# Down projection of a decoder layer: twelve of 22 feature blocks of each half as Strassen products

## The chip, the cores and the metric

The kernel runs on one core of a Trainium2 chip. The engines are named as the profile names them: PE (TensorE, matmuls), DVE (VectorE), ACT (ScalarE), POOL (GpSimd) and SP (the queue that issues most loads). The metric is the device time of one execution in microseconds (us).

## The reference

One decoder layer on 256 tokens of width 2048, float32 throughout: two attention groups side by side, then a feed-forward part of width 5632 and a final norm. The change is in the last product, `@ w_down`.

```python
    x = x + jnp.concatenate([o_mla, o_nsa], axis=-1) @ w_o[l]
    h = rmsnorm(x, ffn_norm_g[l])
    x = x + (jax.nn.silu(h @ w_gate[l]) * (h @ w_up[l])) @ w_down[l]
return rmsnorm(x, final_norm_g)
```

## The kernel before, in words

Products of float32 are made of three matmuls of `float32r` values: each operand is a pair (hi, lo), and hi x hi, hi x lo and lo x hi are added up in a PSUM bank. Weights come as tiles of 128 x 1024 float32. The class `Stream` handles them in the order in which PE takes them: `_dma` loads a tile on SP's queue into `wraw` (three buffers), `_split` copies it on ACT into `whi` (L143) and subtracts that copy from the tile on DVE into `wlo` (L145). In the attention part POOL takes the last 256 columns of the subtraction (L147, `W.share = 256`); from the feed-forward part on DVE takes all of it (`W.share = 0`). A split is one or two tiles ahead of PE.

The feed-forward part runs in two halves of 22 blocks of 128 features (`NFH = 22`). In a half, gate and up are made for each block (`gate_up`, L214 and L215), and `activate` turns their banks into silu(gate) * up, split into `aT`. Then the down projection of that half runs over four column groups `dg` of 512 columns. A weight tile holds two feature blocks x 512 columns; a group takes 11 tiles, and each tile has 12 matmuls of 512 columns (two token halves t, two feature blocks, three products; L856 to L858). The two banks of a group are added to x on DVE (L873). In the second half each finished group is squared and multiplied by `gfin` on POOL (L879); for the last group the second token half is held back by four tiles, so that the first one's output is under way while PE still works.

PE's order is written out by hand in `program()`. The orders on the other engines are set by a scheduler; each engine works its queue in order.

## Time and profile before

| | |
|---|---|
| Median of the runs shown (three) | 1088.46 us (1087.44 to 1089.93) |
| Span of the profiled execution | 1087.1 us, 16200 instructions |
| First and second down projection | 119.72 us and 120.77 us |
| PE busy over the span | 1061.6 us, 98% |
| DVE, ACT, POOL busy over the span | 645.5, 563.3 and 203.8 us |

The profiled execution's own time stands only as its span; the median lies 1.4 us above it. A group of instructions is given by its line, engine, operation, the tiles written and read, its shape, count, busy time and mean duration in ns. Matmuls are pipelined, so a matmul's duration is longer than the time from one start to the next; the pace is read from counts in a window.

### The profile page before, as it was taken

To read this page: it belongs to the slowest core of one execution; us is meant where nothing else is said; L and a number is where in the kernel's file an instruction comes from. 1 tells how busy PE (TensorE), PEld (TensorE's weight loads), DVE (VectorE), ACT (ScalarE), POOL (GpSimd) and SP (SyncE) were. 2 spreads that over 40 slices of the span, in tenths; PEclk is the share of its full clock that TensorE was granted. 3 is DMA by queue.
4 is the path that set the end of the run, shared out by engine and by line. 5 is a ranking of instruction groups with operands and counts; after the bars stand their busy time and mean duration, and the time that the engine had idled before them with its cause. 6 is when DMAs were issued, how large, how long until landed. Compare 5 with 4: busy or idle time off the path is not lost.

```text
span 1087.1 us, 16200 instructions
## 1 busy us (share of the span) xinstructions
PE 1061.6 (98%) x6102; PEld 927.9 (85%) x6102; DVE 645.5 (59%) x1016; ACT 563.3 (52%) x993; POOL 203.8 (19%) x206
## 2 busy tenths in 40 slices
PE   7989999899999999999999999999999999999996
PEld 7989998778888888888888888888888888888885
DVE  4557989886556555555555544455555555555554
ACT  5647887854455544454544333344444444444442
POOL 1144444533343010101011000001010010101110
PEclk9989999999999999999999999999999999999999
DMA  8844443324456555555555555555555555556553
GB/s 275 268 136 157 142 133 98 99 97 135 136 169 214 187 187 192 193 191 185 190 191 193 193 194 194 194 186 184 194 179 189 186 186 191 182 189 193 194 194 134
DMA packets 54543, 193.57 MB, mean 178 GB/s; under 512 B 6404, under 2 KB 6660, under 8 KB 54336
## 3 DMA queue, kind: packets, MB, share of 16 engines
q1 hardware_dynamic: 54000, 191.36, 53.6%
q0 software_dynamic: 464, 1.17, 0.3%
q8 instruction: 48, 0.79, 0.3%
q14 instruction: 31, 0.25, 0.1%
HBM read 190.41 MB, written 2.10 MB: 177 GB/s over the span
## 4 chain that ended last, share of the span: by engine, by line
PE 89%; DVE 4%; ACT 3%; issue 1%; DMA 1%; SPq 0%; POOL 0%; POOLq 0%; DVEq 0%; ACTq 0%
PE up L214 15%; PE gate L214 15%; PE gate L215 8%; PE up L215 8%; PE dn L857 7%; PE dn L858 7%; PE dn L856 7%; PE woM L745 1%; PE woM L746 1%; PE woM L747 1%; PE woN L745 1%; PE woN L747 1%; PE woN L746 1%; PE ps_q L219 1%; DVE wlo L145 1%
## 5 line engine op out<-in xcount | busy, mean ns | idle before, releaser
L145 DVE TENSOR_TENSOR wlo<-wraw,whi 128x1024 fp32r<-128x1024 f32 (+3 forms) x351 | 417.0, 1188 | 386.6 <-ACT whi L143 385.4
L143 ACT CAST whi<-wraw 128x1024 fp32r<-128x1024 f32 (+2 forms) x351 | 366.1, 1043 | 448.1 <-PE dn L858 127.8
L214 PE MATMUL gate<-h2T,whi 128*128 128x512 f32 x704 | 248.7, 395 | 0.0
L214 PE MATMUL up<-h2T,whi 128*128 128x512 f32 x704 | 248.5, 395 | 0.0
L215 PE MATMUL gate<-h2T,wlo 128*128 128x256 f32 x704 | 197.7, 281 | 0.0
L215 PE MATMUL up<-h2T,wlo 128*128 128x256 f32 x704 | 197.7, 281 | 0.0
L824 POOL TENSOR_TENSOR u<-t,RB 128x512 f32<-128x512 f32 x44 | 57.0, 1296 | 556.7 <-DVE t L823 556.7
L214 PEld LDWEIGHTS up<-h2T,whi 128*128 128x128 f32 x704 | 132.0, 187 | 30.8
L214 PEld LDWEIGHTS gate<-h2T,whi 128*128 128x128 f32 x704 | 132.0, 188 | 30.7
L857 PE MATMUL dn<-wlo,aT 128*128 128x512 f32 x352 | 137.2, 390 | 0.6 <-DVE wlo L145 0.6
L858 PE MATMUL dn<-whi,aT 128*128 128x512 f32 x352 | 137.1, 390 | 0.0
L856 PE MATMUL dn<-whi,aT 128*128 128x512 f32 x352 | 137.1, 389 | 0.0
L215 PEld LDWEIGHTS gate<-h2T,wlo 128*128 128x128 f32 x704 | 133.2, 189 | 0.1
L215 PEld LDWEIGHTS up<-h2T,wlo 128*128 128x128 f32 x704 | 133.2, 189 | 0.0
L147 POOL TENSOR_TENSOR wlo<-wraw,whi 128x256 fp32r<-128x256 f32 x70 | 88.6, 1266 | 143.2 <-ACT whi L143 118.2
L857 PEld LDWEIGHTS dn<-wlo,aT 128*128 128x128 f32 x352 | 66.1, 188 | 14.7 <-DVE wlo L145 1.0
L856 PEld LDWEIGHTS dn<-whi,aT 128*128 128x128 f32 x352 | 66.1, 188 | 13.8
L858 PEld LDWEIGHTS dn<-whi,aT 128*128 128x128 f32 x352 | 66.1, 188 | 13.6
L219 PE MATMUL ps_q<-hT,whi 128*128 128x256 f32 x128 | 38.1, 297 | 0.5 <-ACT RB L210 0.5
L220 PE MATMUL ps_q<-hT,whi 128*128 128x256 f32 x128 | 36.7, 287 | 0.0
L221 PE MATMUL ps_q<-hT,wlo 128*128 128x256 f32 x128 | 36.7, 287 | 0.0
L745 PE MATMUL woN<-whi,oT 128*128 128x512 f32 x64 | 26.7, 417 | 0.2 <-ACT oT L548 0.2
(322 smaller groups left out, 1491.6 us busy)
## 6 DMA issues: line engine op xcount, KB each, us to landing
wraw<-in_w_dram SPq DMA_DIRECT2D x338, 512.0 KB, 3.5
wraw<-in_g_dram SPq DMA_DIRECT2D x15, 440.0 KB, 5.0
x<-in_x_dram SPq DMA_DIRECT2D x4, 512.0 KB, 5.6
out_dram<-x SPq DMA_DIRECT2D x8, 256.0 KB, 2.6
xt<-in_xT_dram SPq DMA_DIRECT2D x3, 512.0 KB, 5.3
gfin<-in_gfin_dram POOLq DMA_DIRECT2D x1, 1024.0 KB, 5.9
xt<-in_xT_dram SPq DMA_DIRECT2D x1, 384.0 KB, 5.4
cst<-in_c_dram SPq DMA_DIRECT2D x1, 320.0 KB, 4.5
```

Of the source, the lines that this page charges most:

```text
L143: nc.scalar.copy(hi[:, c0:c1], raw[:, c0:c1])
L145: nc.vector.tensor_sub(lo[:, c0:c2], raw[:, c0:c2], hi[:, c0:c2].bitcast(F32))
L147: nc.gpsimd.tensor_sub(lo[:, c2:c1], raw[:, c2:c1], hi[:, c2:c1].bitcast(F32))
L214: nc.tensor.matmul(ps[0:hi.shape[1], :], hi, act, start=start, stop=False)
L215: nc.tensor.matmul(ps[0:hi.shape[1], 0:S], lo, act[:, 0, :], start=False, stop=stop)
L219: nc.tensor.matmul(ps, hi, act[:, 0, :], start=start, stop=False)
L220: nc.tensor.matmul(ps, hi, act[:, 1, :], start=False, stop=False)
L745: nc.tensor.matmul(pts[t], h_, wh, start=first, stop=False)
L824: nc.gpsimd.tensor_mul(u, t2, RB[:, None, :].to_broadcast([P, 2, S]))
L856: nc.tensor.matmul(pts[t], h_, wh, start=f == 0, stop=False)
L857: nc.tensor.matmul(pts[t], h_, wl, start=False, stop=False)
L858: nc.tensor.matmul(pts[t], l_, wh, start=False, stop=f == NFH - 1)
```

## The change

Of the 22 feature blocks of each half, blocks 0 to 11 become three steps of four blocks. A step takes the activations of its four blocks as a 2 x 2 arrangement A (token half x pair of blocks) and two column groups of the weights as a 2 x 2 arrangement B (pair of blocks x column group). The four block products of a step used to be eight products of a 128-token half with a weight tile; now they are seven, with four sums of weight tiles (P1 to P4) and four sums of activations (s1 to s4). Three of the weight sums are made on POOL, P2 on DVE. The sums are then split into hi and lo as loaded tiles are. Blocks 12 to 21 stay plain; their matmuls go into the same banks as the products. A pass `p` covers two column groups, and the eight banks are one set m1 to m8, of which m1, m5, m6 and m7 are combined with each other (`combine`) and all are added to x. The eight banks are in use in every pass. `whi` has four buffers instead of three, the tiles of the feed-forward part five instead of three; the sums have three of their own. `oT` moves to the pool of the attention part to make room. In the second half gate uses the banks S0 and O. The `gfin` tile is loaded in the second half.

```diff
+NS = 3
+UNITS = ("B11", "P1", "P3", "P2", "B22", "P4", "B21")
+LOADS = {"B11": (0, 0), "P1": (0, 1), "P3": (1, 1), "P4": (1, 0)}
+SUMS = {"P1": ("B11", "B12"), "P3": ("B12", "B22"), "P2": ("P1", "B22"), "P4": ("P2", "B21")}
+RAW_OF = {"B11": "B11", "P1": "B12", "P3": "B22", "P4": "B21"}
+A11, A12, A22, S1, S2, S3, S4 = range(7)
+PLAIN = (2, 4), (3, 8)
+PRODUCT = {"B11": (A11, 1), "P1": (S1, 5), "P3": (S3, 7), "P2": (S2, 6), "B22": (S4, 3), "P4": (A22, 4), "B21": (A12, 2)}
+def down_units(h, p):
+    plain = [("w", ("down", h, 2 * p + c, j)) for j in range(2 * NS, NFH // 2) for c in range(2)]
+    s = []
+    for i in range(NS):
+        for u in UNITS:
+            s.append(("sw", u, h, p, i))
+            if u in (("B11",) if i == NS - 1 else ("B11", "P1", "P2")):
+                s.append(plain.pop(0))
+    return s + plain
...
-        s += [("w", ("down", h, dg, j)) for dg in range(4) for j in range(NFH // 2)]
+        s += [u for p in range(2) for u in down_units(h, p)]
...
+            pool, tag, bufs = self.raws
+            if i - bufs in self.live:
+                return
...
+    def _sum(self, upto):
+        while self.na < min(upto, len(self.units)):
+            u = self.units[self.na]
+            if u[0] == "w":
+                self.parts[self.na] = self._take()
+            else:
+                what, at = u[1], u[2:]
+                if what in RAW_OF:
+                    r = RAW_OF[what]
+                    self.parts[at, r, "i"], self.parts[at, r] = self._take()
+                if what in SUMS:
+                    x, y = (self.parts[at, n] for n in SUMS[what])
+                    t = self.parts[at, what] = self.pool.tile([P, 1024], F32, tag="wraw", name=f"{what}_{self.na}", bufs=3)
+                    eng = self.nc.vector if what == "P2" else self.nc.gpsimd
+                    eng.tensor_add(t, x, y)
+                    if what == "P3":
+                        self._spent(at, "B12")
+                self.parts[self.na] = None, self.parts[at, what]
+            self.na += 1
...
-                    hi, lo = (self.pool.tile([P, 1024], F32R, tag=f"w{n}", name=f"w{n}{i}", bufs=3)
...
+                hi = self.pool.tile([P, 1024], F32R, tag="whi", name=f"whi{i}", bufs=4)
+                lo = self.pool.tile([P, 1024], F32R, tag="wlo", name=f"wlo{i}", bufs=3)
...
+        self._dma(self.nr + self.DMA_AHEAD)
+        self._sum(i + (self.SUM_AHEAD if unit[0] == "sw" else self.SPLIT_AHEAD))
...
+    NN = NFH - 4 * NS
+    aN = fp.tile([P, NN, 2, S], F32R, name="aN")
+    aS = fp.tile([P, NS, 2, 2, 7, P], F32R, name="aS")
+    W.raws = (fp, "raw", 5)
...
+        one, two = st["a", f % 4 - 2], v
+        a11, a21, a12, a22 = one[:, 0:P], one[:, P:S], two[:, 0:P], two[:, P:S]
+        c = temp(f"c_{h}_{f}").rearrange("p (b s) -> p b s", b=4)
+        s1, s2, s3, s4 = (c[:, b, :] for b in range(4))
+        nc.gpsimd.tensor_sub(s1, a22, a21)
+        nc.gpsimd.tensor_sub(s3, a11, a21)
+        nc.gpsimd.tensor_add(s2, a11, s1)
+        nc.gpsimd.tensor_sub(s4, a12, s2)
+        dst = aS[:, f // 4, f % 2]
+        split(dst[:, 0, A11, :], dst[:, 1, A11, :], a11)
+        split(dst[:, 0, A12:A22 + 1, :], dst[:, 1, A12:A22 + 1, :], two.rearrange("p (b s) -> p b s", b=2))
+        split(dst[:, 0, S1:, :], dst[:, 1, S1:, :], c)
...
+        W.DMA_AHEAD = 5
+        if h == 1:
+            gfin = hp.tile([P, D], F32, tag="big", name="gfin")
+            nc.gpsimd.dma_start(gfin, a["gfin"])
+        for p in range(2):
+            two = bank2(f"m67_{h}{p}")
+            tags = ("S0", "O", "ds", "ds") if h == 0 else ("ds", "ds", "S0", "O")
+            m = {6: two[:, 0, :], 7: two[:, 1, :]}
+            m |= {n: bank(t, f"m{n}_{h}{p}") for n, t in zip((1, 5, 3, 4), tags)}
+            m |= {n: bank("PT", f"m{n}_{h}{p}") for n in (2, 8)}
+            cols = [slice((2 * p + c) * 512, (2 * p + c + 1) * 512) for c in range(2)]
...
+                    h_, l_ = left(k)
+                    nc.tensor.matmul(m[to], h_, wh, start=first and k == 0, stop=False)
+                    nc.tensor.matmul(m[to], h_, wl, start=False, stop=False)
+                    nc.tensor.matmul(m[to], l_, wh, start=False, stop=last and k == 1)
...
+            def combine():
+                e, u, v, w = (temp(f"e{n}_{h}{p}") for n in range(4))
+                nc.scalar.copy(e, m[1])
+                nc.gpsimd.tensor_add(x11, x11, e)
+                nc.vector.tensor_sub(u, e, m[6])
+                nc.vector.tensor_add(w, u, m[5])
+                nc.gpsimd.tensor_sub(x12, x12, w)
+                nc.vector.tensor_add(u, u, m[7])
+                nc.vector.tensor_add(v, u, m[5])
+                nc.gpsimd.tensor_add(x21, x21, u)
+                nc.gpsimd.tensor_sub(x22, x22, v)
...
+                if unit[0] == "sw":
+                    form, to = PRODUCT[unit[1]]
+                    i = unit[4]
+                    mms(to, w, lambda k: [aS[:, i, k, b, form, :] for b in range(2)])
+                    if unit[1] == "B21" and i == NS - 1:
+                        combine()
...
+            if not end:
+                for xs, b in ((x11, 2), (x21, 4), (x12, 3), (x22, 8)):
+                    nc.vector.tensor_add(xs, xs, m[b])
+                if h == 1:
+                    for t in range(2):
+                        final(t, (2 * p, 2 * p + 1))
+                continue
```

POOL's queue at the turn from gate and up to the first down projection. `u` is the activation's product with the row scales, `P1` to `P4` are weight sums with the unit's number, `wraw` are loaded tiles. Before:

```order
L824 TENSOR_TENSOR u_0_19_6248<-t2_0_19_6247,RB_70 128x512
L824 TENSOR_TENSOR u_0_20_6350<-t2_0_20_6349,RB_70 128x512
L824 TENSOR_TENSOR u_0_21_6452<-t2_0_21_6451,RB_70 128x512
L824 TENSOR_TENSOR u_1_0_7360<-t2_1_0_7359,RB_70 128x512
L824 TENSOR_TENSOR u_1_1_7462<-t2_1_1_7461,RB_70 128x512
```

That is the whole of POOL's queue there: from one half's last activation straight to the next half's first. The same place in POOL's queue now:

```order
L905 TENSOR_TENSOR u_0_20_6405<-t2_0_20_6404,RB_70 128x512
L198 TENSOR_TENSOR P3_182_6561<-wraw180_6484,wraw182_6527 128x1024
L198 TENSOR_TENSOR P4_186_6605<-P2_183_6563,wraw184_6543 128x1024
L905 TENSOR_TENSOR u_0_21_6507<-t2_0_21_6506,RB_70 128x512
L198 TENSOR_TENSOR P1_190_6659<-wraw185_6575,wraw187_6633 128x1024
L198 TENSOR_TENSOR P3_192_6701<-wraw187_6633,wraw189_6657 128x1024
L198 TENSOR_TENSOR P4_196_6745<-P2_193_6703,wraw191_6683 128x1024
L198 TENSOR_TENSOR P1_200_6799<-wraw192_6715,wraw194_6773 128x1024
L198 TENSOR_TENSOR P3_201_6813<-wraw194_6773,wraw195_6775 128x1024
L198 TENSOR_TENSOR P4_204_6857<-P2_202_6845,wraw196_6797 128x1024
L1000 TENSOR_TENSOR x_69<-x_69,e0_00_6913 128x512
L1003 TENSOR_TENSOR x_69<-x_69,e3_00_6916 128x512
```

Between the last blocks' activations and after them stand sums of 1024 columns, nine in a pass, and then the sums of `combine` (L1000 to L1007), where there was nothing until the next half's activations.

DVE's queue in the same pass, at the second and third step. `wlo` is the result of a split. Before, splits alone:

```order
L145 TENSOR_TENSOR wlo187_6611<-wraw187_6590,whi187_6610 128x1024
L145 TENSOR_TENSOR wlo188_6629<-wraw188_6608,whi188_6628 128x1024
L145 TENSOR_TENSOR wlo189_6647<-wraw189_6626,whi189_6646 128x1024
L145 TENSOR_TENSOR wlo190_6669<-wraw190_6644,whi190_6668 128x1024
L873 TENSOR_TENSOR x_69<-x_69,dn0_0_6463 128x512 x2
L145 TENSOR_TENSOR wlo191_6687<-wraw191_6666,whi191_6686 128x1024
```

Each split follows the one before, with the evictions of a group (L873) in between. DVE's queue now, from the second step's sum P2 to the third step's first split:

```order
L198 TENSOR_TENSOR P2_193_6703<-P1_190_6659,wraw189_6657 128x1024
L224 TENSOR_TENSOR wlo190_6686<-P1_190_6659,whi190_6685 128x1024
L224 TENSOR_TENSOR wlo191_6706<-wraw188_6635,whi191_6705 128x1024
L224 TENSOR_TENSOR wlo192_6720<-P3_192_6701,whi192_6719 128x1024
L224 TENSOR_TENSOR wlo193_6736<-P2_193_6703,whi193_6735 128x1024
L224 TENSOR_TENSOR wlo194_6748<-wraw190_6671,whi194_6747 128x1024
L224 TENSOR_TENSOR wlo195_6758<-wraw189_6657,whi195_6757 128x1024
L224 TENSOR_TENSOR wlo196_6778<-P4_196_6745,whi196_6777 128x1024
L224 TENSOR_TENSOR wlo197_6788<-wraw191_6683,whi197_6787 128x1024
L198 TENSOR_TENSOR P2_202_6845<-P1_200_6799,wraw195_6775 128x1024
L224 TENSOR_TENSOR wlo198_6802<-wraw192_6715,whi198_6801 128x1024
```

The sum P2 of the next step stands ahead of the split of that step's first tile, and it reads `P1_200`, a sum that POOL makes.

SP's queue over the same loads, in the order of issue; `wraw189` is B22 of the second step, `wraw194` is B12 of the third:

```order
L167 DMA wraw189_6657<-in_w_dram 128x1024
L167 DMA wraw190_6671<-in_w_dram 128x1024
L167 DMA wraw191_6683<-in_w_dram 128x1024
L167 DMA wraw192_6715<-in_w_dram 128x1024
L167 DMA wraw193_6717<-in_w_dram 128x1024
L167 DMA wraw194_6773<-in_w_dram 128x1024
L167 DMA wraw195_6775<-in_w_dram 128x1024
L167 DMA wraw196_6797<-in_w_dram 128x1024
```

There are five buffers, so `wraw194` takes the one that `wraw189` had.

## Rows read from the trace of the kernel before

**Rows 1.** The page: part 1, two rows of part 2, part 4.

```profile
PE 1061.6 (98%) x6102; PEld 927.9 (85%) x6102; DVE 645.5 (59%) x1016; ACT 563.3 (52%) x993; POOL 203.8 (19%) x206
...
PEclk9989999999999999999999999999999999999999
...
PE 89%; DVE 4%; ACT 3%; issue 1%; DMA 1%; SPq 0%; POOL 0%; POOLq 0%; DVEq 0%; ACTq 0%
```

**Rows 2.** Busy time by stage; then of the down projection's instructions (tile dn).

```profile
core 0: us, PE busy (x) PEld busy (x) DVE busy (x) ACT busy (x) POOL busy (x), PEclk, DMA share, GB/s
...
356.70:589.78 233.08, 233.08 (x1348) 205.70 (x1347) 134.10 (x169) 116.53 (x171) 27.32 (x21) 1.00 0.58 190
...
589.78:709.50 119.72, 119.72 (x531) 99.17 (x529) 58.74 (x54) 47.30 (x47) 1.29 (x1) 1.00 0.59 194
...
958.23:1079.00 120.77, 120.20 (x530) 98.87 (x528) 60.62 (x57) 50.23 (x60) 10.96 (x8) 1.00 0.55 180
1079.00:1087.10 8.10, 0.03 (x1) 0.00 (x0) 2.54 (x6) 1.45 (x3) 0.55 (x1) 0.75 0.48 184
...
589.78:709.50 119.72, 119.72 (x528) 98.98 (x528) 4.15 (x7) 1.00 0.59 194
958.23:1079.00 120.77, 120.20 (x528) 98.87 (x528) 4.54 (x7) 1.00 0.55 180
```

**Rows 3.** Waits of the second half of the run: total us, times, longest us.

```profile
DVE wlo L145 <- ACT whi L143: 225.0, 170, 2.8
...
ACT whi L143 <- PE dn L858: 127.8, 78, 1.7
...
PE dn L857 <- DVE wlo L145: 0.6, 1, 0.6
```

**Rows 4.** Groups by line and shape; then durations min/median/max, ns, of L145 and L147.

```profile
L145 DVE TENSOR_TENSOR wlo<-wraw,whi 128x1024 fp32r<-128x1024 f32 x264 | 329.8, 1250 | 328.4 <-ACT whi L143 328.4
...
L873 DVE TENSOR_TENSOR x<-x,dn 128x512 f32<-128x512 f32 x16 | 10.4, 684 | 5.8 <-PE dn L858 5.8
...
L143 ACT CAST whi<-wraw 128x1024 fp32r<-128x1024 f32 x334 | 351.1, 1051 | 437.3 <-PE dn L858 127.8 <-PE gate L214 88.4 <-PE up L214 81.3
...
L824 POOL TENSOR_TENSOR u<-t,RB 128x512 f32<-128x512 f32 x44 | 57.0, 1296 | 556.7 <-DVE t L823 556.7
...
L145 DVE TENSOR_TENSOR wlo<-wraw,whi x259: 1217/1226/2056, 355.0 to 1069.7; 128x1024 fp32r<-128x1024 f32 x130
...
L147 POOL TENSOR_TENSOR wlo<-wraw,whi x70: 724/1508/1562, 48.6 to 339.5; 128x256 fp32r<-128x256 f32 x70
```

**Rows 5.** Timeline at 301 us, DVE, then POOL: start, duration, instruction.

```profile
301.20 0.96 DVE L145 TENSOR_TENSOR wlo<-wraw,whi 128x768 fp32r<-128x768 f32 x1 [1.14 <-ACT whi L143]
302.07 0.55 DVE L549 TENSOR_TENSOR mpl<-mpt,mph 128x384 fp32r<-128x384 f32 x1
...
301.24 1.51 POOL L147 TENSOR_TENSOR wlo<-wraw,whi 128x256 fp32r<-128x256 f32 x1 [2.73 <-ACT whi L143]
```

**Rows 6.** Timeline at 1050 us, in the last half, DVE, then POOL.

```profile
1052.10 2.05 DVE L145 TENSOR_TENSOR wlo<-wraw,whi 128x1024 fp32r<-128x1024 f32 x1 [1.43 <-ACT whi L143]
1054.82 1.23 DVE L145 TENSOR_TENSOR wlo<-wraw,whi 128x1024 fp32r<-128x1024 f32 x1 [0.67 <-ACT whi L143]
...
1050.01 3.06 POOL L879 TENSOR_TENSOR x<-x,gfin 128x512 f32<-128x512 f32 x2 [26.96 <-ACT fsq L877]
```

**Rows 7.** Loads of weight tiles in the down projection (issue ns, us to landing).

```profile
L122 SPq DMA_DIRECT2D wraw<-in_w_dram x37: 327/328/328, 600.6 to 698.4; - x37
...
DMA to landing us min/median/max: 3.4/3.4/4.8
```

**Rows 8.** Busy time around 60 us (the eighth column is PEclk); PE's wait there.

```profile
56.00:59.00 3.00, 0.74 (x7) 0.53 (x5) 2.94 (x8) 2.82 (x7) 2.07 (x5) 1.00 0.32 130
59.00:66.00 7.00, 6.20 (x29) 6.23 (x30) 4.69 (x12) 2.02 (x5) 1.41 (x2) 0.51 0.18 49
...
59.80 3.59 PE L388 MATMUL ps_hk<-bl_k,wraw 128*128 128x32 f32 x16 [3.06 <-POOL wlo L147]
```

More of the change, by code (lines that the diff above doesn't have):

```diff
@@ L87, in program, with loads @@
                 s += w(*A("gate", f), *A("up", f))
-        s += [("w", ("down", h, dg, j)) for dg in range(4) for j in range(NFH // 2)]
+        s += [u for p in range(2) for u in down_units(h, p)]
     return s
+def loads(step):
+    if step[0] == "w":
+        return [step[1]]
+    if step[0] == "sw" and step[1] in LOADS:
+        u, h, p, i = step[1:]
+        r, c = LOADS[u]
+        return [("down", h, 2 * p + c, 2 * i + r)]
+    return []
 def plan():
-    return [k[1] for k in program() if k[0] == "w"]
+    return [k for s in program() for k in loads(s)]
 def width(key):
@@ L123, in _dma, with _take, _spent @@
             self.raw[i] = t
+            self.live.add(i)
             self.nd += 1
+    def _take(self):
+        i = self.nr
+        self.nr += 1
+        self._dma(i + 1)
+        return i, self.raw.pop(i)
+    def _spent(self, at, *names):
+        for n in names:
+            self.live.discard(self.parts.pop((at, n, "i")))
+    def _sum(self, upto):
[17 more added lines that the diff above has]
+            self.na += 1
@@ L126, in _split @@
     def _split(self, upto):
         nc = self.nc
-        while self.ns < min(upto, len(self.order)):
-            i = self.ns
-            self._dma(i + 1)
-            raw = self.raw.pop(i)
-            if self.order[i][0] in ("w1k", "w1v"):
+        while self.ns < min(upto, len(self.units)):
+            i, u = self.ns, self.units[self.ns]
+            self._sum(i + 1)
+            n, raw = self.parts.pop(i)
+            if u[0] == "w":
+                self.live.discard(n)
+            elif u[1] in ("B11", "B22", "B21"):
+                self._spent(u[2:], u[1])
+            if u[0] == "w" and u[1][0] in ("w1k", "w1v"):
@@ L790, in gate_up @@
         if j == 0:
-            st[n, f] = bank("ds" if n == "gate" else "PT", f"{n}{f}")
+            tag = "PT" if n == "up" else "ds" if f < NFH else ("S0", "O")[f % 2]
+            st[n, f] = bank(tag, f"{n}{f}")
         for kk in range(8):
@@ L797, in layer_kernel @@
     while step[0] == "w":
[L798 removed]
+        gate_up(step[1], W.get(*step))
         step = next(steps)
@@ L840, in layer_kernel @@
                 done += 1
-        for dg in range(4):
-            if dg % 2 == 0:
-                dn = bank2(f"dn{h}_{dg}")
-                pts = [dn[:, 0, :], dn[:, 1, :]]
-            else:
-                pts = [bank("S0", f"dn{h}_{dg}_0"), bank("O", f"dn{h}_{dg}_1")]
-            last = h == 1 and dg == 3
-            ntile = NFH // 2
-            def down(t, j, w):
+        W.DMA_AHEAD = 5
+        if h == 1:
+            gfin = hp.tile([P, D], F32, tag="big", name="gfin")
+            nc.gpsimd.dma_start(gfin, a["gfin"])
@@ new lines, in layer_kernel, with mms @@
+        for p in range(2):
[5 more added lines that the diff above has]
+            cols = [slice((2 * p + c) * 512, (2 * p + c + 1) * 512) for c in range(2)]
+            x11, x12, x21, x22 = (x[:, t, c] for t in range(2) for c in cols)
+            todo = down_units(h, p)
+            uses = [b for u in todo for b in ((PRODUCT[u[1]][1],) if u[0] == "sw" else PLAIN[u[1][2] % 2])]
+            total = {b: uses.count(b) for b in m}
+            count = dict.fromkeys(m, 0)
+            def mms(to, w, left):
@@ L851, in down @@
                 hi, lo = w
+                first, last = count[to] == 0, count[to] == total[to] - 1
+                count[to] += 1
                 for k in range(2):
[L853 removed]
                     wh, wl = hi[:, k * 512:(k + 1) * 512], lo[:, k * 512:(k + 1) * 512]
[L855 to L857 removed]
@@ new lines, in layer_kernel @@
+            end = h == 1 and p == 1
+            held = []
+            for n, unit in enumerate(todo):
+                assert next(steps) == unit
+                w = W.get(*unit)
+                if unit[0] == "sw":
[5 more added lines that the diff above has]
+                    continue
+                plain(0, unit[1], w)
+                if end and n >= len(todo) - 3:
+                    held.append((unit[1], w))
+                else:
+                    plain(1, unit[1], w)
@@ new lines, in layer_kernel @@
+            if not end:
[4 more added lines that the diff above has]
+                        final(t, (2 * p, 2 * p + 1))
+                continue
+            nc.vector.tensor_add(x11, x11, m[2])
+            nc.vector.tensor_add(x12, x12, m[3])
+            final(0, (2 * p, 2 * p + 1))
+            for b in range(2):
+                for key, w in held:
+                    if key[2] % 2 == b:
+                        plain(1, key, w)
+                nc.vector.tensor_add((x21, x22)[b], (x21, x22)[b], m[4 if b == 0 else 8])
+                final(1, (2 * p + b,))
```

124 lines of the change are left out of this document (55 added, 69 removed).

## The prediction

> **What bounds the kernel now.** I read the page first. PE is busy 98% of the span, the granted clock stands at full speed in nearly every slice, and the chain that ended last is 89% PE [rows 1]. So the next question is whether PE ever waits in the stage that changes. By stages, the two halves of the down projection take 119.72 and 120.77 us; PE is busy in all of the first and all but 0.57 us of the second, with 528 matmuls in each [rows 2]. That is 119.72 / 528 = 0.2267 us from one matmul of 512 columns to the next. From the waits of that stretch the reader sees that everybody else waits for PE: the hi copies on ACT stood 127.8 us behind matmuls that had yet to free a buffer, the splits on DVE stood behind ACT, and PE itself waited 0.6 us, once [rows 3]. DVE is busy 58.74 of 119.72 us and POOL 1.29 [rows 2]. The stage is PE alone, so fewer matmuls would shorten it one for one, as long as whoever prepares the weights keeps up. The change buys fewer matmuls with more prepared weights, so the profile has to be read once more from that side.
>
> **What PE saves.** I call one pass over two column groups of one half a quarter; there are four. Before, a quarter is 2 groups x 11 tiles x 12 matmuls = 264. Now it has 21 products of 6 matmuls and 10 plain tiles of 12, together 246. That is 72 fewer in all, worth 72 x 0.2267 = 16.3 us if PE stays the bound. PE's own time for a quarter falls from 59.85 to 55.8 us.
>
> **What the preparation costs.** A quarter now has 31 tiles to split instead of 22, because the weight sums P1 to P4 are split like loaded tiles, and it makes 12 sums.
> - DVE: 31 splits, 1.226 us each (the median; the mean by form has stalled ones in it), and three P2 sums, which have the same size, so I take the same 1.226 [rows 4]. 34 x 1.226 = 41.7 us. Eight sums that read a PSUM bank are new or moved, four in combine and four evictions, 0.68 us each [rows 4]: 5.4 us.
> - ACT: 31 copies x 1.05 + 0.6 = 33 us, under any of the limits here [rows 4].
> - POOL: nine sums of 1024 columns and four of 512. The trace has no POOL sum of 1024. With nobody in its way POOL takes 0.724 us for 256 columns and 1.296 for 512 [rows 4], so 0.572 per 256, and 1.296 + 2 x 0.572 = 2.44 us for 1024. Bounds: not under 1.30 (the 512 row), not over 2.59 (twice it). I take 2.44, on the line through both rows. 9 x 2.44 + 4 x 1.30 = 27.2 us.
>
> Each engine alone is under 55.8 us, so by separate queues PE would stay the bound. They are not separate. In rows 5 a split and POOL's part of the same split start within 0.04 us of each other; DVE takes its usual 0.96 for 768 columns and is done at 302.16, POOL ends at 302.75, 1.51 us for work that takes 0.724 alone. POOL got 0.59 us of it, all after DVE had ended. The reverse is in rows 6, on different tiles: POOL's two products end at 1053.07, a split that started at 1052.10 takes 2.05 us instead of 1.226 and ends 1.08 us after POOL. Whoever is second waits for the other's whole instruction. It is the usual case: the median of POOL's 70 such parts is 1.508 us [rows 4]. An operation that reads PSUM is not held: at 302.07, beside POOL, one takes its 0.55 [rows 5].
>
> The Trainium skill has two versions. Its page Advanced Engine Details and Errata (VectorE Performance Modes) lets POOL instructions and DVE instructions in a two-port mode block each other; a split has two tensors and no such mode, so by that note alone the splits would run on, and the time would be that of the first rival below. Its page SBUF — State Buffer (SBUF: two separate sides) adds DVE operations with two SBUF inputs against a POOL operation that reads SBUF, for the whole instruction; rows 5 and 6 agree with that one. Its GPSIMD Engine Reference (Elementwise) gives 4497 ns for a sum of 2048 columns; an estimate from it, half, is 2.25 us, which would make my sum 4 x 9 x 0.19 = 6.8 us shorter.
>
> So the work that excludes each other has to be added up. A quarter: 41.7 + 27.2 = 68.9 us. A handover gives a little back: 0.724 - 0.59 = 0.13 on POOL, 1.226 - 1.08 = 0.15 on DVE, say 0.14, twice for each of 13 POOL operations: 3.6. That leaves 65.3 us, against PE's 55.8 now and 59.85 before. **The stage changes its bound from PE to the pair DVE and POOL**, and the saved matmuls are worth nothing.
>
> To this come stretches in which neither can work:
> - The raw tiles have five buffers. In the third step the tile B12 reuses the buffer of B22 of the step before (`wraw194` of `wraw189`), whose last reader is the split `wlo195`. A load lands 3.4 us after its issue [rows 7]; P1 on POOL needs it, and the P2 sum, which stands in the DVE queue ahead of the next tile's split, needs P1. Between stand two splits, 2.5 us: 1.0 us idle, and behind that P2 sum wait three splits for which PE has nothing else. PE, two or three tiles ahead, runs dry for some 4 us there.
> - Two of the four PSUM sums in combine fall between splits while POOL waits for their result: 2 x 0.68 = 1.4. The rest run beside POOL.
> - P4 needs P2's sum on DVE, then 2.44 on POOL, then 1.05 on ACT, with one or two splits to cover it: about 1 us, in the third step.
>
> I take 3.5 of these, within 0 and 9 (all PSUM sums bare, and the others): a quarter is 69 us, within 65 and 74. At the turn from one quarter to the next DVE stands with its P2 sum ahead of the evictions of m4, m3 and m8, so banks are late by a POOL sum too; it is inside the same queue and not added. In the second half the four gfin products of the last-but-one pair (4 x 1.30 = 5.2) now fall into a full pair; before, they stood under PE [rows 6]. The quarters are 69, 69, 69 and 74: 281 us. Each half begins with two sums and a split made under the gate stage (about -6), but also with the last block's activation, now in the same pair (1.30 + 3 x 0.42), and it ends with PE working off three plain tiles (+3). I call that even. 281 - 240.5 = +40.5.
>
> **The rest at nothing.** In the gate stages an activation adds up to four small POOL operations and two splits per block; DVE is busy 134 of 233 us there and POOL 27 [rows 2], and their results are read no sooner than the down stage. If that cover were gone, 12 blocks would show up to 2 us each. The tail after the last matmul, 8.1 us [rows 2], keeps its chain (eviction, square, power, scaling, store). The moved gfin load is read a quarter later.
>
> **The sum.** The profiled span is 1087.1 us; the median of the runs shown is 1088.46, 1.4 above. 1087.1 + 40.5 = 1127.6, and with the 1.4, **1129 us**. A change within 0.2% (2 us) cannot be told from none.
>
> **The rivals.**
> - *The pair does not exclude each other for these sums*, PE stays the bound: 984 matmuls x 0.2267 = 223.1, and about 1 us of bank waits at each of four quarters: 240.5 - 227 = -13, 1075 us, faster. For it: three separate queues that all fit. Against it: rows 5 and 6, and 1.508 as a median. It decides where a quarter's pair time falls under 59.85: 5.4 us less, a POOL sum of 1.84 instead of 2.44.
> - *The sums hide better than I count*, with the handover gains, no idle stretches and short POOL sums near 2.25: quarters of 64 to 66, about +20, 1109 us. For it: DVE and POOL always find something queued. Against: the chain B12, P1, P2 in one row.
> - *The clock falls as well.* When PE had been busy 0.74 of 3.0 us, after a wait of 3.06, the granted clock was 0.51 over the next 7 us, 1.2 GHz for nearly all of it [rows 8]. Here PE runs dry for about 4 us at least once a quarter. Seven us at half speed cost 3.5 us of PE, eight times 28 us; PE has 13 us to spare in a quarter, but not in the third step. If none is absorbed: 1157 us; half of it, 1143.
> - *It nets to nothing*: needs quarters of 60, between the first two.
>
> **How the numbers follow.** Pair-bound as summed, 1117 to 1140: 0.66. Hiding better, 1096 to 1117: 0.13. With the clock, 1140 to 1160: 0.13. PE-bound, faster: 0.06. Nothing: 0.02. The range leaves out the last two and the far ends: 1102 to 1152. Faster 0.06, same 0.02, slower 0.92.
>
> **What would show it.** Right: in the down stages PE is busy under 85%, its waits end on the splits (wlo) and hi copies, the means of the POOL sums and of the splits lie 0.5 us or more above 2.4 and 1.23, and the stages take 135 to 145 us each. The longest PE waits stand at the third step's B11. Wrong: PE at 98% in the down stages; POOL sums of 2.4 us beside splits of 1.23 that overlap them in the timeline; or a POOL sum far from 2.44.

## The result, and the profile after

| | before | after |
|---|---|---|
| Median | 1088.11 us (4 runs) | 1119.31 us (4 runs, 1119.06 to 1120.7) |
| Ratio | | 1.0294, 95% interval 1.0275 to 1.0313 |
| Span of the profiled execution | 1087.1 us | 1118.9 us (its own time 1120.7) |
| Start of the first down stage | 589.78 | 584.84 |
| The two down stages | 119.72 and 120.77 | 139.36 and 137.19 |
| After the last matmul | 8.10 | 8.76 |

The kernel became slower by 2.9%, as forecast in sign, by 31.8 us of span where 40.5 were forecast. The stages between the two halves take the same time (248.73 before, 248.75 after), so the difference is made of three parts: -4.9 ahead of the first down stage, +36.1 in the two down stages, +0.7 at the end.

Busy times of the whole page first, then the four quarters by windows (columns as in [rows 2]).

```profile
PE 1062.7 (95%) x6030; PEld 918.4 (82%) x6030; DVE 798.5 (71%) x1090; ACT 608.3 (54%) x1047; POOL 382.9 (34%) x304
...
584.84:653.40 68.56, 61.27 (x252) 48.48 (x251) 60.38 (x45) 34.27 (x36) 35.17 (x14) 0.95 0.52 164
653.40:724.20 70.80, 61.22 (x243) 48.55 (x243) 58.56 (x43) 32.28 (x32) 32.06 (x13) 0.93 0.51 166
972.95:1040.00 67.05, 60.02 (x252) 47.53 (x251) 60.23 (x44) 34.39 (x38) 34.90 (x15) 0.97 0.53 181
1040.00:1110.14 70.14, 60.51 (x244) 46.54 (x242) 61.43 (x46) 34.39 (x43) 42.73 (x18) 0.95 0.38 127
```

A quarter was about 60 us, and in all four PE was idle for 0.57 us [rows 2]. Now it is 67 to 71, PE is busy 60 or 61 of them, and neither DVE (59 to 61) nor POOL (32 to 43) fills it alone: by this table nobody is the bound. Added, DVE and POOL come to 91 to 104 us in 67 to 71. Two independent engines could show that sum too, so it proves nothing yet; whether they take turns has to be read from single instructions. The waits of PE in the down stages, in all, number and longest:

```profile
PE m L990 <- DVE wlo L224: 32.2, 21, 3.6
PE m L989 <- DVE x L1028: 1.0, 2, 0.7
```

Before, one wait of 0.6 us stood there [rows 3]. The groups of the first down stage (POOL's sums, DVE's splits of loaded tiles and of sums, DVE's P2 sum), and behind them the durations of POOL's sums, min/median/max in ns:

```profile
L198 POOL TENSOR_TENSOR P<-wraw,wraw 128x1024 f32<-128x1024 f32 x11 | 32.6, 2970 | 41.3 <-DMA wraw<-in_w_dram 34.4 <-issue 7.0
...
L224 DVE TENSOR_TENSOR wlo<-wraw,whi 128x1024 fp32r<-128x1024 f32 x39 | 56.2, 1455 | 7.2 <-PE m L990 3.4 <-issue 3.3
L224 DVE TENSOR_TENSOR wlo<-P,whi 128x1024 fp32r<-128x1024 f32 x24 | 40.2, 1693 | 6.2 <-PE m L990 3.5 <-issue 2.3
L198 DVE TENSOR_TENSOR P<-P,wraw 128x1024 f32<-128x1024 f32 x5 | 13.7, 2741 | 6.6 <-POOL P L198 4.6 <-DMA wraw<-in_w_dram 2.0
...
L198 POOL TENSOR_TENSOR P<-wraw,wraw x24: 2367/3056/3452, 576.2 to 1082.3; 128x1024 f32<-128x1024 f32 x24
L198 POOL TENSOR_TENSOR P<-P,wraw x12: 2386/3312/3392, 590.5 to 1089.3; 128x1024 f32<-128x1024 f32 x12
```

Ten of the 36 POOL sums take 2.37 to 2.42 us, and 22 take 3.0 to 3.45. A P2 sum on DVE, an operation of the size of a split (1.226 in [rows 4]), takes 2.74 in the mean of the first down stage. That the extra is time spent standing behind the other engine is seen in the timeline. The timeline of the third step, DVE, then POOL, then PE (start, duration, instruction, idle time before it and what ended it):

```profile
624.90 3.37 DVE L198 TENSOR_TENSOR P<-P,wraw 128x1024 f32<-128x1024 f32 x1 [2.29 <-POOL P L198]
628.19 2.35 DVE L224 TENSOR_TENSOR wlo<-wraw,whi 128x1024 fp32r<-128x1024 f32 x2
630.46 2.39 DVE L224 TENSOR_TENSOR wlo<-P,whi 128x1024 fp32r<-128x1024 f32 x2
...
621.72 5.47 POOL L198 TENSOR_TENSOR P<-wraw,wraw 128x1024 f32<-128x1024 f32 x2 [6.86 <-DMA wraw<-in_w_dram]
...
629.46 0.80 PE L990 MATMUL m<-wlo,aS 128*128 128x512 f32 x1 [3.64 <-DVE wlo L224]
```

Read it from the second block: POOL waits for B12's load, makes P1 and P3 one behind the other until 627.19; DVE's P2 sum, which needs P1, starts in the middle, shows 3.37 us, and ends at 628.27, 1.08 us after POOL; only then comes the split of the third step's B11, and PE has been dry for 3.64 us. That end is no accident: in the two down stages a POOL instruction ends in the course of 44 splits and P2 sums on DVE, and every one of the 44 ends 1.08 to 1.11 us after it, the time of one such operation (1.22) less 0.11 to 0.14, however long before it had started.

### The profile page after: what moved, and what is told of

It reads as the page before. It is cut to its first block, busy times and chain, and to the rows that moved or that the text cites. A ratio compares the mean times of both kernels' runs of the same rounds, so it can differ in the third digit from the quotient of the medians.

```text
span 1118.9 us, 16555 instructions
## 1 busy us (share of the span) xinstructions
PE 1062.7 (95%) x6030; PEld 918.4 (82%) x6030; DVE 798.5 (71%) x1090; ACT 608.3 (54%) x1047; POOL 382.9 (34%) x304
## 5 line engine op out<-in xcount | busy, mean ns | idle before, releaser
L224 DVE TENSOR_TENSOR wlo<-wraw,whi 128x1024 fp32r<-128x1024 f32 (+3 forms) x339 | 424.8, 1257 | 212.1 <-PE up L294 77.8
L222 ACT CAST whi<-wraw 128x1024 fp32r<-128x1024 f32 (+2 forms) x339 | 354.3, 1045 | 339.5 <-issue 124.3
L905 POOL TENSOR_TENSOR u<-t,RB 128x512 f32<-128x512 f32 x44 | 61.8, 1404 | 347.5 <-DVE t L904 347.5
L198 POOL TENSOR_TENSOR P<-wraw,wraw 128x1024 f32<-128x1024 f32 x24 | 70.9, 2961 | 91.2 <-DMA wraw<-in_w_dram 84.2
L990 PE MATMUL m<-wlo,aS 128*128 128x512 f32 x168 | 69.2, 412 | 25.7 <-DVE wlo L224 25.4
L224 DVE TENSOR_TENSOR wlo<-P,whi 128x1024 fp32r<-128x1024 f32 x48 | 83.8, 1765 | 12.0 <-PE m L990 6.8
L222 ACT CAST whi<-P 128x1024 fp32r<-128x1024 f32 x48 | 50.0, 1048 | 60.2 <-POOL P L198 35.1
L990 PE MATMUL m<-wlo,aN 128*128 128x512 f32 x160 | 66.7, 417 | 6.8 <-DVE wlo L224 6.8
L991 PE MATMUL m<-whi,aS 128*128 128x512 f32 x168 | 67.4, 401 | 0.0
L989 PE MATMUL m<-whi,aN 128*128 128x512 f32 x160 | 66.0, 413 | 1.0 <-DVE x L1028 1.0
L989 PE MATMUL m<-whi,aS 128*128 128x512 f32 x168 | 66.4, 395 | 0.0
L991 PE MATMUL m<-whi,aN 128*128 128x512 f32 x160 | 65.0, 406 | 0.0
L990 PEld LDWEIGHTS m<-wlo,aS 128*128 128x128 f32 x168 | 32.4, 193 | 39.1 <-DVE wlo L224 32.9
```

Of the source, the lines that this page charges most:

```text
L198: eng.tensor_add(t, x, y)
L222: nc.scalar.copy(hi[:, c0:c1], raw[:, c0:c1])
L224: nc.vector.tensor_sub(lo[:, c0:c2], raw[:, c0:c2], hi[:, c0:c2].bitcast(F32))
L905: nc.gpsimd.tensor_mul(u, t2, RB[:, None, :].to_broadcast([P, 2, S]))
L989: nc.tensor.matmul(m[to], h_, wh, start=first and k == 0, stop=False)
L990: nc.tensor.matmul(m[to], h_, wl, start=False, stop=False)
```

## The experiments

Theory A is the prediction's: DVE and POOL exclude each other, and their added work is the bound. Theory B: the exclusion matters little, and it is waiting (loads, chains, buffers) that costs.

**Take POOL's sums away.** P1, P3 and P4 are copies of their first operand, made by ACT, instead of sums made by POOL. This kernel leaves the sums out, so it multiplies by other weights than the layer's; it is there for its time alone.

```diff
-                    eng = self.nc.vector if what == "P2" else self.nc.gpsimd
-                    eng.tensor_add(t, x, y)
+                    if what == "P2":
+                        self.nc.vector.tensor_add(t, x, y)
+                    else:
+                        self.nc.scalar.copy(t, x)
```

> P1, P3 and P4 are copies of their first operand, made on ACT, so the product steps use other weights than the reference's; queues, tiles, units and buffers stay. Theory A (DVE and POOL exclude each other): without the nine sums a quarter of the down projection has 34 x 1.23 + 4 x 1.30 = 46.9 us of pair work against 55.8 of PE and 42 of ACT, so PE is the bound again: both down stages together 223 to 232 us instead of 276.5, the run 1067 to 1076 us, the mean of the splits in the stage back at 1.23 to 1.3. Theory B (the order is what costs: a raw tile lands late, P2 stands ahead of the next splits in the queue): the waits at the third step stay, both stages over 250 us, the run over 1093.

Measured: 1074.03 us, ratio 0.9886 (0.9864 to 0.9907). Windows of the two down stages:

```profile
584.87:697.14 112.27, 111.90 (x495) 92.27 (x493) 92.51 (x85) 82.19 (x83) 16.27 (x9) 1.00 0.61 200
945.87:1063.14 117.27, 113.63 (x494) 91.55 (x492) 94.68 (x87) 84.06 (x96) 24.73 (x15) 1.00 0.51 175
```

The same loads, the same order, buffers, splits and matmuls, and PE is busy in 111.90 of 112.27 us in the first half and 113.63 of 117.27 in the second. The stages take 229.5 us together, 11.0 less than before, of the 16.3 that the matmuls were to bring. All of the loss goes with POOL's sums. One thing more goes with them: a copy reads one operand, so P1 no longer waits for B12's load nor P4 for B21's, and a copy of 1.05 us makes the chain from P1 over P2 to P4 shorter too.

**All sums on DVE.** One line: `self.nc.vector.tensor_add(t, x, y)`.

> All twelve weight sums of a quarter on DVE, none on POOL. Theory A: pair work 43 x 1.226 = 52.7, the four x sums on POOL 4 x 1.16, and 3 to 5 us of sums from PSUM that stand bare: 60 to 63 us a quarter, 240 to 252 for the four, the run 1083 to 1095 us: a sum costs half as much on DVE as on POOL when the two exclude each other. Theory B: three more sums stand in the same queue as the splits and behind the same landing tile, so it gets slower than 1119.

Measured: 1092.64 us, ratio 1.0045 (1.0027 to 1.0062).

```profile
584.88:707.53 122.65, 115.17 (x495) 91.34 (x494) 111.10 (x102) 66.81 (x67) 27.40 (x9) 1.00 0.59 187
956.25:1081.80 125.55, 116.18 (x494) 92.31 (x492) 115.28 (x105) 69.20 (x80) 29.32 (x15) 0.99 0.52 168
...
PE m L989 <- DVE wlo L223: 15.5, 15, 1.9
```

Giving 36 sums to the engine that is already busier than POOL saves 28 us of the two stages, and here every sum still waits for both of its loads: a sum costs DVE 1.2 us and would cost the pair 2.4 on POOL. Two engines side by side are worth less than one here. The run lies in theory A's range; theory B had forecast a slower one. What this edit does not take apart is exclusion and latency, since a sum on DVE also ends sooner. That is decided by the count of busy time further down.

**One more raw buffer,** for the 1.0 us that the prediction put on B12's landing: `W.raws = (fp, "raw", 6)`, `W.DMA_AHEAD = 6`.

> Six buffers for loaded tiles instead of five, and loads six ahead: the second column group's tile B12 of the third step no longer waits for the split of B22. Theory A: only the idle time of the pair at the third step goes, 1 to 2 us a quarter: 1111 to 1116 us. Theory B: the landing is what PE waits for there; the waits of 3.6 us go and most of the stage's loss with them: under 1105.

Measured: 1119.74 us, ratio 1.0299 (1.0275 to 1.0323): no gain. Both theories missed. POOL, then DVE, in the third step:

```profile
618.69 2.40 POOL L198 TENSOR_TENSOR P<-wraw,wraw 128x1024 f32<-128x1024 f32 x1 [2.45 <-DMA wraw<-in_w_dram]
625.66 3.42 POOL L198 TENSOR_TENSOR P<-wraw,wraw 128x1024 f32<-128x1024 f32 x1 [4.57 <-DMA wraw<-in_w_dram]
...
618.74 4.57 DVE L224 TENSOR_TENSOR wlo<-wraw,whi 128x1024 fp32r<-128x1024 f32 x2 [0.28 <-issue]
...
625.63 1.23 DVE L198 TENSOR_TENSOR P<-P,wraw 128x1024 f32<-128x1024 f32 x1 [1.18 <-DMA wraw<-in_w_dram]
626.77 5.67 DVE L224 TENSOR_TENSOR wlo<-wraw,whi 128x1024 fp32r<-128x1024 f32 x3
```

P1 does start 3 us earlier (618.69 for 621.72), but two splits that come up with it on DVE now take 4.57 instead of 2.35, P3 and P2 wait for the next load, and the three splits behind them take 5.67. The idle time of one moment only changed its place: the pair stands idle for 19.6 us in the two stages, 18.3 in the change (the table below).

**The two side edits on the kernel before.** The change also has a fourth hi buffer, and to make room puts oT among the attention tiles; the kernel before with these two alone.

```diff
-                    hi, lo = (self.pool.tile([P, 1024], F32R, tag=f"w{n}", name=f"w{n}{i}", bufs=3)
+                    hi, lo = (self.pool.tile([P, 1024], F32R, tag=f"w{n}", name=f"w{n}{i}", bufs=4 if n == "hi" else 3)
```

> The kernel before with the two edits of the change that are not in the down projection: four hi buffers instead of three, and oT in the attention pool. If these make the 4.9 us that the part ahead of gate and up lost with the change: 1082 to 1085 us, with gate starting near 339.6 us. If that is chance or another order of the instructions: 1087 to 1090.

Measured: 1084.04 us, ratio 0.9963 (0.9951 to 0.9976). The stretch of [rows 8] in this kernel, and then in the change:

```profile
56.00:59.00 3.00, 3.00 (x23) 3.00 (x23) 2.61 (x7) 2.09 (x6) 2.00 (x5) 0.83 0.21 85
59.00:66.00 7.00, 7.00 (x58) 6.48 (x57) 6.42 (x15) 3.70 (x9) 2.17 (x3) 1.00 0.44 147
```

```profile
56.00:59.00 3.00, 2.58 (x23) 2.41 (x21) 2.95 (x8) 2.80 (x7) 2.21 (x5) 1.00 0.04 15
59.00:66.00 7.00, 7.00 (x58) 6.48 (x57) 5.45 (x14) 3.58 (x9) 1.97 (x4) 1.00 0.43 150
```

PE's wait of 3.06 us and the 7 us at a granted clock of 0.51 behind it are gone from both: 58 matmuls in these 7 us for 29 before. Here the down stages start at 585.73 and 954.18 (589.78 and 958.23 before). Some 4 of the 4.9 us ahead of the first down stage are the side edits'.

**Fewer steps.** `NS = 2`, sums as in the change; `NS = 2` with all sums on DVE; `NS = 1`. If the pair is one resource and PE another, and the longer sets the quarter, PE is the bound again.

> Two Strassen steps a quarter instead of three (8 of 22 blocks of each half); nothing else changes. Theory A (the pair DVE and POOL is one resource, PE the other, the longer one sets the quarter): PE needs 252 x 0.2267 = 57.1 us a quarter; the pair 30 operations of DVE x 1.226 + 6 sums of POOL x 2.40 + 4 x 1.30, less 10 times two handovers of 0.14, = 53.6, and 5.2 more in the last quarter. PE is the bound again but for the last quarter; with up to 3 us of idle a quarter the two down stages take 230 to 240 us together, against 276.5 with three steps and 240.5 before, the whole 1073 to 1083 us, faster than before. Theory B (each step costs its own stall, whatever the load: (276.5 - 240.5) / 3 = 12 us a step): stages of 264.5 us, 1107 us.

> Two Strassen steps a quarter and all eight sums on DVE. Theory A: PE 57.1 us a quarter; the pair 36 operations of DVE x 1.226 = 44.1, and POOL's four small ones 5.2, together 49.3 and 4 us of margin more than with the sums on POOL; DVE by itself 44.1 + 8 x 0.68 = 49.5. PE is the bound with 8 us to spare: stages of 228.4 to 235 us, 1071 to 1078 us. Theory B (a stall for each step): by the 248.2 us of three steps with the sums on DVE, (248.2 - 240.5) x 2/3 = 5.1, stages of 245.6 us, 1088 us.

> One Strassen step a quarter, sums on POOL as in the change. Theory A: PE 258 x 0.2267 = 58.5 us a quarter, the pair 26 x 1.226 + 3 x 2.40 + 4 x 1.30 = 44.3: PE is the bound by far, stages of 234 to 238 us, 1077 to 1081 us, slower than two steps only by what PE saves less, if two steps are PE-bound too. Theory B: stages of 252.5 us, 1095 us.

Measured: 1107.89 us (ratio 1.0173, 1.016 to 1.0186), 1086.25 (0.9978, 0.9967 to 0.9989) and 1095.50 (1.0059, 1.0046 to 1.0072); down stages of 263.9, 241.9 and 250.6 us. They lie at or near theory B's numbers (264.5, 245.6, 252.5), and not in A's ranges (230 to 240, 228 to 235, 234 to 238). Theory A in this form falls. Windows of two steps on POOL: 23 us from the start of the first half, which hold the first step and the start of the second, and then a stretch among the plain tiles at the end of either of its quarters.

```profile
584.92:608.00 23.08, 18.71 (x81) 14.48 (x79) 19.75 (x15) 12.24 (x14) 11.25 (x5) 1.00 0.46 139
631.00:641.00 10.00, 10.00 (x46) 8.29 (x45) 4.90 (x4) 4.22 (x4) 0.00 (x0) 1.00 0.71 234
697.00:713.00 16.00, 16.00 (x73) 13.24 (x72) 8.24 (x8) 6.34 (x6) 0.00 (x0) 1.00 0.68 217
```

In the first stretch DVE and POOL together show 31.0 us and PE lacks 4.4. In the other two PE is busy throughout, POOL not at all and DVE half the time. The pair has time to spare there, but a split can be made only two or three tiles ahead (three lo buffers, four hi), so it is not to be had where it is missing. I call that distance the lead. That gave a theory A2: the pair is the bound, over a stretch as short as the lead.

**One hi buffer less** in the change (`bufs=3`).

> The change with three hi buffers, as before it, instead of four; three steps, sums on POOL. Theory A: the 3.06 us wait of PE near 57 us and the half-speed spell behind it come back, and with them most of the 4.9 us ahead of the first gate stage: 1121 to 1124 us, the down stages as they were (276 to 278 us, since the pair and not the buffers sets them). Theory B (the fourth buffer carries the down stages): these grow by 5 us or more.

Measured: 1139.90 us, ratio 1.0471 (1.0458 to 1.0485), 20 us more than the change. PE's wait near 57 us is back (first line, of 50 to 70 us) and the first down stage starts at 589.78 again, though oT keeps its new place, so the 4.9 us are the fourth buffer's; but the down stages grew too, by 13.1 us, which theory A did not expect.

```profile
PE ps_hk L469 <- POOL wlo L226: 3.1, 1, 3.1
...
589.78:733.90 144.12, 121.33 (x495) 94.72 (x493) 122.47 (x88) 67.31 (x68) 66.39 (x26) 0.95 0.49 157
982.63:1128.15 145.52, 123.30 (x494) 94.61 (x492) 124.97 (x89) 70.46 (x81) 77.52 (x32) 0.95 0.45 146
```

```profile
ACT whi L222 <- PE m L991: 116.0, 102, 7.0
```

The second fence is ACT's longest wait in the down stages, for a hi buffer that PE has yet to free: 116.0 us, 80.9 in the change. DVE and POOL together have nearly as much work as in the change (260.2 us for 258.2, the table below); with one tile less of lead they stand idle 11 us longer.

**The same tiles in another order.** Two steps again, plain tiles between the products:

```diff
-            if u in (("B11",) if i == NS - 1 else ("B11", "P1", "P2")):
+            if u != "P3" and (i, u) != (NS - 1, "B21"):
                 s.append(plain.pop(0))
```

and for three steps `if u in ("P1", "P4") or (i, u) == (1, "B21"):`.

> As the run with two steps and sums on POOL, but the plain tiles stand between the products, six and five to a step and three at the end, instead of three, one and ten. Same instructions, another order. Theory A2 (the pair DVE and POOL is the bound locally: the sums of one step come in a burst, the two or three tiles that lie ready are all the lead there is, and pair time left over beside the last ten plain tiles is lost): a step with six plain tiles needs 7 x 1.36 + 6 x 2.72 = 25.8 us of PE and 14 x 1.226 + 3 x 2.40 - 0.84 = 23.5 of the pair, so PE sets it: down stages of 228.4 to 236 us against 263.9 clustered, 1071 to 1079 us in all. Theory B2 (each step has a chain of its own, B12, P1, P2, P4, that costs its latency wherever the plain tiles stand): stages of 258 us or more, 1102 to 1108 us.

> The same order with all eight sums on DVE. Theory A2: a step needs 25.8 us of PE and 13 splits and 4 sums, 17 x 1.226 = 20.8, of DVE, 2.7 less than with POOL: stages of 228.4 to 233 us against 241.9 clustered, 1071 to 1076 us. Theory B2: stages as clustered, 240 us or more, 1084 to 1088 us.

> The change with three steps and its sums on POOL, seven plain tiles spread two, three and two over the steps (after P1 and P4) instead of three, three and one. Theory A2: the pair has 65 us of work a quarter against 55.8 of PE, in every step more than PE, and no order of the same work shortens it: stages of 268 to 280 us against 276.5, 1111 to 1122 us. Theory B2's opposite (the order makes the stall, not the sum of the work): stages under 262 us, under 1105 us.

Measured: 1091.34 us (ratio 1.0026, 1.0014 to 1.0038), 1086.39 (0.9985, 0.9974 to 0.9996) and 1116.71 (1.0261, 1.0244 to 1.0278); down stages of 245.4, 239.7 and 272.0 us.

- Two steps on POOL: 18.5 us less than clustered, with not an instruction taken away. That speaks against B2, a latency of each step wherever the plain tiles stand (258 us or more). But it is 9 us more than A2's range. And not all of the 18.5 need be the pair's: the rows below, the two halves clustered and then spread, have PEclk at 0.97 and 0.95, then at 1.00 and 0.99. By an estimate from them some 20 us ran at half speed clustered and 3 spread, which can be worth 9 us of PE's time.
- Three steps: inside A2's range. Where the pair is overfull in every step, order gives 4.5 of 276.5 us.
- Two steps on DVE: a miss of A2 (228.4 to 233 us), and the time lies in B2's range (1084 to 1088 us); order gave 2.2 us of the stages. By halves the two theories part: the first is A2's (116.38 us, PE busy 115.79), the second takes 123.31 (the last two rows below).

```profile
584.92:716.16 131.24, 119.61 (x506) 96.45 (x505) 103.98 (x79) 60.63 (x61) 48.21 (x20) 0.97 0.56 177
964.89:1097.58 132.69, 121.89 (x506) 98.22 (x504) 100.94 (x84) 64.04 (x76) 58.44 (x25) 0.95 0.50 159
...
585.69:706.02 120.33, 115.80 (x507) 94.13 (x506) 101.94 (x79) 60.83 (x61) 48.65 (x20) 1.00 0.61 194
954.74:1079.81 125.07, 117.72 (x506) 95.15 (x504) 101.09 (x81) 62.88 (x74) 59.45 (x26) 0.99 0.51 169
...
586.62:703.00 116.38, 115.79 (x507) 94.21 (x506) 99.38 (x89) 60.72 (x61) 18.03 (x9) 1.00 0.61 200
951.73:1075.04 123.31, 117.12 (x506) 95.22 (x504) 98.78 (x91) 63.10 (x74) 28.01 (x15) 0.99 0.52 171
```

The lead shows in DVE's waits for PE to free a lo buffer, clustered and then spread, with the sums on POOL (total us, times, longest):

```profile
DVE wlo L224 <- PE m L990: 38.2, 26, 3.4
...
DVE wlo L224 <- PE m L990: 12.6, 10, 1.5
```

Part of what is left of the run with two steps spread on POOL stands at the start of a half. POOL, then DVE, and 10 us later POOL and DVE again:

```profile
584.11 3.38 POOL L198 TENSOR_TENSOR P<-wraw,wraw 128x1024 f32<-128x1024 f32 x1 [2.63 <-DMA wraw<-in_w_dram]
585.48 2.30 DVE L630 TENSOR_TENSOR aN<-u,aN 128x256 fp32r<-128x256 f32 x1
...
593.35 3.11 POOL L198 TENSOR_TENSOR P<-P,wraw 128x1024 f32<-128x1024 f32 x1 [5.85 <-DMA wraw<-in_w_dram]
...
598.20 0.42 DVE L908 TENSOR_TENSOR u<-sl,u 128x256 f32<-128x256 f32 x1 [3.99 <-ACT sl L906]
```

The last block's activation is done here among the first sums. An operation of 0.42 us takes 2.30 behind a POOL sum, and DVE's queue stands for 3.99 us for an ACT result that needs a product on POOL (L905); that product stands in POOL's queue behind a sum that waits 5.85 us for its load.

**The load of gfin later.** In the second half of the last version the longest wait of PE (3.2 us) goes back to a P sum that waited 5.31 us for a raw tile, beside the 1 MB load of gfin. The lines that issue that load were put at the twentieth tile of the third quarter.

> As the run with two steps spread and all sums on DVE, but the 1 MB load of gfin is issued in the middle of the third quarter (at its twentieth tile) instead of at the start of the second half. In that run the second half took 123.31 us against 116.38 of the first; the longest wait of PE in it, 3.15 us, stands behind a P sum on DVE that waited 5.31 us for a raw tile whose load ran beside that of gfin, and the granted clock was at half speed for some 3 us behind it. Theory: the two loads share the DMA engines; with gfin out of the way the wait goes, and with it the half-speed spell: 3.2 + 1.7 us less, the second half 118 to 120 us, 1080.5 to 1083 us in all, 0.5 to 0.7% faster than before. Rival: the late raw tile is the fault of its own buffer order, or the load merely does the same harm elsewhere: 123 us, 1085.5 to 1087 us.

Measured: 1084.87 us, ratio 0.9973 (0.9962 to 0.9983); second half 123.38 us. The theory's time (1080.5 to 1083 us) did not come, but it was not put to the test: the only wait ahead of the issue is 8.43 us for PE, and it went out 0.46 us after the start of the down stage, as in the run without the edit. POOL, then DVE in the second half and at the same place in the first:

```profile
951.41 0.65 POOL L1012 DMA_DIRECT2D gfin<-in_gfin_dram  x1 [8.43 <-PE up L293]
...
960.13 1.23 DVE L197 TENSOR_TENSOR P<-P,wraw 128x1024 f32<-128x1024 f32 x1 [5.25 <-DMA wraw<-in_w_dram]
...
590.77 1.55 DVE L197 TENSOR_TENSOR P<-P,wraw 128x1024 f32<-128x1024 f32 x1 [0.97 <-DMA wraw<-in_w_dram]
```

The same sum waits 0.97 us in the half without the load and 5.25 in the half with it. That they collide is likely, and not shown; a load held back by something it has to wait for was not tried.

## Why the prediction was right, and where its numbers were off

I put the runs into one table. PE's need is the matmuls times 0.2267. The pair's busy time is worked out from the traces' starts and ends: every POOL operation and every DVE operation that doesn't take a PSUM bank of the down projection, in the two down stages, overlaps counted once and cut at the stages' ends; the rest is the pair's idle time.

| | down stages | PE's need | pair busy | pair idle |
|---|---|---|---|---|
| the change | 276.6 | 223.1 | 258.2 | 18.3 |
| six raw buffers | 275.1 | 223.1 | 255.5 | 19.6 |
| three hi buffers | 289.6 | 223.1 | 260.2 | 29.4 |
| three steps, spread | 272.0 | 223.1 | 254.9 | 17.1 |
| sums on DVE | 248.2 | 223.1 | 220.2 | 28.0 |
| two steps | 263.9 | 228.5 | 214.5 | 49.4 |
| two steps, spread | 245.4 | 228.5 | 214.4 | 31.0 |
| two steps, spread, on DVE | 239.7 | 228.5 | 190.3 | 49.4 |
| one step | 250.6 | 234.0 | 169.4 | 81.2 |
| no sums on POOL (ACT copies) | 229.5 | 223.1 | 185.2 | 44.4 |

**The mechanism was right.** The bound moved from PE to the pair: busy 93% of the two stages, so by this count no order and no buffer could, with three steps, bring the stages much under 255 us. The pair's work is nearly the same in every order and with any buffers (255 to 260 with three steps, 214 with two), which is what one shared resource looks like, and the single instructions show the turns being taken. Each step adds 44 to 45 us over the four quarters and saves PE 5.4. For three steps this settles theory A against a mere latency of POOL's sums. With two steps the pair is not full over the stage, and what holds the kernel there is argued from A2 and only in part shown.

**Terms, against the chip.** The quarters were forecast as 69, 69, 69 and 74 and took 68.6, 70.8, 67.1 and 70.1: 276.6 for 281. The first three come to 206.4 for 207. The 3.9 us are missing in the last one, where 5.2 stood for the gfin products: the pair is busy 2.7 us longer in the second half than in the first (130.5 for 127.8), but idle for 6.7 instead of 11.6. The work was put at 4 x 65.3 + 5.2 = 266 and is 258, and that is no miss of the sum: 32 of the 36 POOL sums and 10 of the 12 P2 sums start in the stages, the others under gate, as the forecast said. With its own terms for the ends (-6 a half, and +2.6 for the last block's activation) it had 259.5 of work there, and 14 + 6 = 20 idle, for 18.3.

Inside the work, terms are off that offset each other. A POOL sum alone is 2.37 us, neither 2.44 nor the 2.25 of the second estimate. Splits one behind the other start 1.14 us apart (587.08 and 588.22 below), not 1.226; over the two stages such DVE operations overlap by 6.3 us. A handover gives back what was forecast (1.22 - 1.08 = 0.14 on DVE, 2.37 - 2.25 = 0.12 on POOL), but there are 87 of them, not 104. What these take off is more than the 1.3 us by which the whole is off; the rest was not traced.

```profile
587.08 1.21 DVE L224 TENSOR_TENSOR wlo<-wraw,whi 128x1024 fp32r<-128x1024 f32 x1
588.22 1.21 DVE L224 TENSOR_TENSOR wlo<-P,whi 128x1024 fp32r<-128x1024 f32 x1
```

**The step that failed: "the rest at nothing".** I counted nothing for the fourth hi buffer and for oT's new place. Ahead of the down stages they are worth some 4 us (the run on the kernel before), and the buffer alone 4.9 in the change (the run with three of them), by taking away the one wait of [rows 8] and the half-speed spell behind it; I had that row, and used it for a rival only. In the down stages the change would be 13 us slower without the fourth buffer: the sum has no term for the lead, and that four buffers give enough of it to come near 281 was not worked out. So the forecast of 1129 for 1119.3 (span 1127.6 for 1118.9) is off by -4.9 ahead of the first down stage, -4.5 in the stages and +0.7 at the end; the median lies 0.4 above the span of the profiled execution, where 1.4 were added.

**B12's landing was no term.** One more buffer let P1 start 3 us earlier and gave back nothing in the median. Where the pair was overfull, the idle time came back elsewhere.

**The clock.** The rival was half right: the granted clock fell to half speed in every quarter (0.93 to 0.97 in the windows above, for 1.00 before in [rows 2]), behind waits of up to 3.6 us. By an estimate from that column some 27 of the 276.6 us ran at half speed, worth up to 14 us of PE's time, half of what the rival put at eight spells. But all the quarters together came out no longer than the forecast without it; what the slow matmuls added is not told apart from the waits that they stand behind.

**What would show it.** The stages were to take 135 to 145 us and take 139.36 and 137.19. PE was to be busy under 85% and is at 88%: time at half speed counts as busy. POOL's sums lie 0.6 above 2.4, DVE's splits of sums 0.47 above 1.226 but those of loaded tiles only 0.23: the operations beside the sums pay, not all. The longest waits stand at the third step's B11, as said, and last 3.64 us where some 4 were forecast.

**Where the reasoning was too coarse.** It added up a whole quarter. With three steps a quarter is overfull throughout, and the sum came out right. With two, the same sum says 53.6 us for the pair and 57.1 for PE, PE-bound, and the chip took 65.6 and 66.3 a quarter in the means of the two halves. By A2 the bound has to be taken over a stretch as long as the lead, here two or three tiles; the run with two steps spread, 18.5 us faster but 9 over A2's range, bears that out in part.

**What is best.** No version that makes all the sums beats the kernel before with the two side edits alone (0.9963). The versions with two steps and sums on DVE (0.9973 to 0.9985) have these edits too, so their products bring nothing that can be told: down stages of 239.7 us for 239.6 in the kernel with the side edits. The way to the 11 us of the ACT copies is open: sums that cost the pair nothing, or a longer lead. A fourth lo buffer was not tried, though one hi buffer more or less made 13 us in the down stages.

**Left open.** Why the second half takes 7 us more than the first with two steps spread and the sums on DVE, and 5 with the ACT copies (the gfin load, the last activation and the gfin products are all there); what holds two steps 9 us over A2's range; and the last us of the 4.9, which the side edits did not bring in the kernel before.

## What to carry to other kernels

Before work is moved to an idle engine, look in the trace for one pair of instructions that shows it and a busy engine excluding each other; if there is one, add the times of the two. A busy table with nobody over 90% can hide a resource that is full. Take that sum over a stretch as long as the buffers let work run ahead, not over the stage: with two steps, 18.5 of the 35 us lost against PE's need went with the order, some of it through the granted clock. And price every small edit that comes with a change (a buffer count, a tile's place): without the fourth hi buffer the change would have lost 18 us more, and the matmuls saved were worth 16.3.
